# Weight casts ahead of the last square of a chunk, and the plain heads' values split at step 10

## The chip, the cores and the metric

The kernel runs on one core of a Trainium2 chip. The metric is the device time of one execution in microseconds (us). The core has five engines that run side by side and wait for each other through semaphores: TensorE (PE in the profile, its weight loads PEld), VectorE (DVE), ScalarE (ACT), GpSimd (POOL) and SyncE (SP), which here only issues the loads and stores (DMA). Each engine works through its own queue in order, so an instruction that waits holds up all that stands behind it on that engine.

## What is computed

One layer of a transformer block: a modulated norm, one input projection into three groups of heads (plain attention with grouped keys, a long convolution, differential attention), an output projection, and a gated feed-forward part, for 512 latent tokens and 256 context tokens of width 1024. Cut to what matters here:

```python
qa, ka, va, hy, qd, kd, vd = jnp.split(h @ w_in, IN_SPLITS, axis=-1)          # 512 latent rows
qa_c, ka_c, va_c, hy_c, qd_c, kd_c, vd_c = jnp.split(hc @ w_in, IN_SPLITS, axis=-1)  # 256 context rows
ka = apply_rope(rms_norm(ka.reshape(b, n, A_KV_HEADS, HEAD_DIM), kn_a), cos, sin)
qa = apply_rope(rms_norm(qa.reshape(b, n, A_HEADS, HEAD_DIM), qn_a), cos, sin)
ya = gqa_attention(qa, concat([ka_c, ka]), concat([va_c, va]))
yd = diff_attention(qd, concat([kd_c, kd]), concat([vd_c, vd]), lam)   # qd, kd normed and rotated alike
yh = hyena(hy, ...)
y = merge_groups(ya, yh, yd, g_out, w_out, lam_init)
x = x + g1 * y
x = x + g2 * conv_glu(modulate(rms_norm(x, norm2_g), sh2, sc2), w_up, ffn_conv_w, ffn_conv_b, w_down)
```

All is float32. The kernel keeps that accuracy by splitting each operand into a high half (a cast to the matmul's shorter type) and a low half (the operand minus the high half), and by three matmuls for one: high x high, high x low, low x high.

## The kernel before

**The projection.** The weights for queries, keys and values come as 16 units of 128x1024, two for each of eight chunks `ch`, in the order 0, 1, 4, 2, 3, 5, 6, 7 (`ci` counts them). A `Stream` (line 121) loads a unit raw (`wr`, three buffers, SP), casts its high half (`wh`, ScalarE, line 72) and subtracts its low half (`wl`, VectorE, line 80); high and low halves have two buffers each. `get(i)` (line 144) prepares units i and i+1 and loads the next two. So the call for the second half of a chunk prepares units 2ci+1 and 2ci+2, and unit 2ci+3 is prepared by the call at the start of the next chunk. Its buffer is the one of unit 2ci+1, which TensorE reads last in the last matmul of chunk ci.

A chunk fills two banks for the latent rows (`q0L` and so on) and, for keys and values, a third one for the context rows (`q3C`). After its matmuls each bank is evicted (lines 863 to 924): for queries and keys ScalarE squares it (`sq`, line 880) into one of four large buffers `b` that it shares with the rotation's products `ra`, `rb`; VectorE sums the square by head; POOL turns the sum into a reciprocal root and adds and scales the products. Chunks 6 and 7 and a part of 5 are values and are copied.

**Modulation columns.** Beside this, `mod2_step` (line 746) loads 512 KB pieces `mraw` and accumulates them on VectorE (`macc`, line 764); after eight pieces TensorE sums the columns (`mc`, line 769).

**Order of the instructions.** Outside the sections that fix it by hand, a scheduler chooses each engine's order from its own timeline, with the written order and any edges that are added as its limits. `tc.issue_after(ins)` adds such an edge: what is traced inside it comes behind `ins` on the same engine. In chunk 7 the order of TensorE and VectorE is fixed as written, and in the attention (line 1176) that of TensorE, VectorE and ScalarE.

**The attention.** Steps n from 3 to 28: four differential heads with four steps each (a step is 128 queries; its two score tiles of 128x768 are `jj` 0 and 1), then two blocks of plain heads. A step writes, in this order, the scores and maximum of `jj` 0, the mixing of the step before (`combine`: POOL scales and adds), a first `advance()`, the transposes, the exponential and the other half, the value matmuls of five steps before, and a second `advance()`. `advance()` takes each running generator one `yield` further: head preparation (`prepare`, started at the steps in `PREP_AT`), head finishing (`finish_d`), and `split_va` (line 946), which is started at step `VA_AT`. It casts the values of a plain head (`vas` from `va`, 128x768, ScalarE), yields, subtracts the low half on VectorE, yields, and does the same for the second head. The tiles take the place of `kd0` and `kd1`, the keys of the differential heads, which `prepare` reads for the last time in step 9. The score tiles have two buffers, so the scores of a step wait for the exponential of the same half in the step before.

Of the kernel before, what the change touches and what calls it, by code (L numbers as in the profile page):

```python
# [1 line left out]

# [8 lines left out]
AF = mybir.ActivationFunctionType  # L11
# [10 lines left out]
EARLY = 3  # L22
MOD_AT = (0, 0, 0, 2, 2, 2, 2, 2, 2, 2, 2, 2, 2, 2, 0, 0)
PREP_AT = (4, 7, 12, 17)
VA_AT = 13
HY_AT = (5, 6)
WO_AT = (24, 26, 28)
TAIL = (2, 0, 0, 0, 0, 0, 10, 0, 0, 4)
# [16 lines left out]
def block_kernel(tc, x, ctxt, small, ffs, wmod1, wmod2, whyd, wqkvd, woutd, wupd, wdownd,  # L45
                 fw1d, fw2d, fw3d, hbiasd, gains, identd, zTd, decayd, dftd, coefd, roped, out):
    nc = tc.nc
    V, S, G, T_ = nc.vector, nc.scalar, nc.gpsimd, nc.tensor
# [21 lines left out]
    def hi_of(dst, src, eng):  # L70
        if eng == "a":
            return S.copy(dst, src)  # L72
        elif eng == "v":
            V.tensor_copy(dst, src)
        else:
            G.tensor_scalar(dst, src, 1.0, 0.0, ALU.mult, ALU.add)

    def lo_of(dst, src, hi, eng):
        e = V if eng == "v" else G
        return e.tensor_tensor(dst, src, f(hi), ALU.subtract)  # L80
# [27 lines left out]
    def pa(name):  # L108
        return psB.tile([P, 512], F32, tag="a", bufs=3, name=name)
# [8 lines left out]
    def big(name):  # L118
        return tmp.tile([P, 1024], F32, tag="b", bufs=4, name=name)

    class Stream:
# [12 lines left out]
        def prep(self, i):  # L134
            if i < len(self.units) and i not in self.split:
                self.load(i)
                r = self.raw[i]
                h = self.pl.tile([P, 1024], F32R, tag=self.tag + "h", bufs=self.hb, name=f"{self.tag}h{i}")
                l = self.pl.tile([P, 1024], F32R, tag=self.tag + "l", bufs=self.hb, name=f"{self.tag}l{i}")
                hi_of(h, r, self.heng(i))  # L140
                lo_of(l, r, h, self.leng(i))
                self.split[i] = (h, l)

# [50 lines left out]
    def rstd_of(o, ss, n, k):  # L194
        G.tensor_scalar(o, ss, 1.0 / n, EPS, ALU.mult, ALU.add)
        G.tensor_tensor(o, o, mhalf[:, :k], ALU.pow)
# [615 lines left out]
    def early_mix(n):  # L812
        ml = cst.tile([P, 1], F32, tag="mle", bufs=2, name=f"mle{n}")
        mix(held[n], state["rr0"][:, n], state["st0"][:, n], ml)
# [3 lines left out]
    squ = Stream(wp, [wqkvd[2 * c_ + u] for c_ in corder0 for u in range(2)], lambda i: "a", lambda i: "v")  # L818
    corder = (0, 1, 4, 2, 3, 5, 6, 7)
    tabs = {}  # L820
    for ci, ch in enumerate(corder):
        kv = ch in (2, 3, 5, 6, 7)
        banks = [pa(f"q{ch}L0"), pa(f"q{ch}L1")] + ([pa(f"q{ch}C")] if kv else [])
        banks = [Bank(t) for t in banks]
        if ci == 6:
            for _ in prepare(0, pt):
                pass
        for u in range(2):
            for _ in range(MOD_AT[2 * ci + u]):
                mod2_step()  # L830
            if ci == 7 and u == 0:
                order = tc.manual_schedule(engines={mybir.EngineType.PE, mybir.EngineType.DVE})
                order.__enter__()
                nextp = prepare(1, pt)
            wh, wl = squ.get(2 * ci + u)
            wh, wl = (w.rearrange("p (k c) -> p k c", k=4) for w in (wh, wl))
            for b, bank in enumerate(banks):
                th, tl = (hTh, hTl) if b < 2 else (cTh, cTl)
                for j in range(2):
                    tt = (2 * b + j) if b < 2 else j  # L840
                    sl = slice(tt * P, (tt + 1) * P)
                    for kk in range(4):
                        k = 4 * u + kk
                        bank.mm3(bank.t[:, j * 256:(j + 1) * 256], th[:, k, sl], tl[:, k, sl], wh[:, kk], wl[:, kk],
                                 j == 1 and k == NK - 1)
                    if ci == 7:
                        e = 6 * u + 2 * b + j
                        if e % 2 == 0:
                            early_step(e // 2)
                        if e in (4, 8):  # L850
                            early_mix(e // 4 - 1)
                        if e in (2, 4, 6, 8, 9):
                            mod2_step()
                        if e > 3:
                            next(nextp, None)
            if ci == 7 and u == 1:
                for _ in nextp:
                    pass
                early_mix(EARLY - 1)
                while m2s["n"] < m2s["end"] or "due" in m2s:  # L860
                    mod2_step()
                order.__exit__(None, None, None)
        for b, bank in enumerate(banks):
            bank = bank.t
            lat = b < 2
            kt0 = 2 + 2 * b if lat else 0
            bv = bank.rearrange("p (j g d) -> p j g d", j=2, g=4)
            b2 = bank.rearrange("p (j c) -> p j c", j=2)

            if ch in (0, 1, 2, 3, 4, 5):  # L870
                ngr = 2 if ch == 5 else 4
                isq = ch in (0, 1, 4)
                w = ngr * 64
                ti = {0: 2, 1: 2, 2: 3, 3: 3, 4: 0, 5: 1}[ch]
                src = bv[:, :, :ngr, :]
                if ti not in tabs:
                    tabs[ti] = tables(ti)
                t512 = lambda nm: big(f"{nm}{ch}{b}")[:, :2 * ngr * 64].rearrange("p (j g d) -> p j g d", j=2, g=ngr)
                sq = t512("sq")
                S.activation(sq, src, AF.Square)  # L880
                s8 = tmp.tile([P, 2, ngr], F32, tag="s8", bufs=2, name=f"s8{ch}{b}")
                V.tensor_reduce(s8, sq, AX.X, ALU.add)
                r8 = tmp.tile([P, 2, ngr], F32, tag="r8", bufs=2, name=f"r8{ch}{b}")
                rstd_of(r8.rearrange("p j g -> p (j g)"), s8.rearrange("p j g -> p (j g)"), 64, 2 * ngr)
                if isq:
                    G.tensor_scalar(r8, r8, QK_SCALE, 0.0, ALU.mult, ALU.add)
                if isq:
                    dst = (qa[:, 2 * b:2 * b + 2, :] if ch == 4 else qd[:, 2 * b:2 * b + 2, ch * 256:(ch + 1) * 256])
                elif ch == 5:
                    dst = ka[:, kt0:kt0 + 2, :]  # L890
                else:
                    dst = kd[ch - 2][:, kt0:kt0 + 2, :]
                dst4 = dst.rearrange("p j (g d) -> p j g d", d=64)
                r4 = r8.rearrange("p j g -> p j g").unsqueeze(3).broadcast_to([P, 2, ngr, 64])
                if lat:
                    ra, rb = t512("ra"), t512("rb")
                    for tg, tab in zip((ra, rb), tabs[ti]):
                        tb = tab[:, 2 * b:2 * b + 2, :].unsqueeze(2).broadcast_to([P, 2, ngr, 64])
                        V.tensor_tensor(tg, src, tb, ALU.mult)
                    swp = rb.rearrange("p j g (i w) -> p (j g i) w", w=2)[:, :, ::-1]  # L900
                    ras = ra.rearrange("p j g (i w) -> p (j g i) w", w=2)
                    G.tensor_tensor(ras, ras, swp, ALU.add)
                    G.tensor_tensor(dst4, ra, r4, ALU.mult)
                else:
                    ra = t512("rc")
                    gb = gbc[:, ti, :].unsqueeze(1).unsqueeze(1).broadcast_to([P, 2, ngr, 64])
                    V.tensor_tensor(ra, src, gb, ALU.mult)
                    G.tensor_tensor(dst4, ra, r4, ALU.mult)
            if ch == 5:
                if b == 0:  # L910
                    for i in range(2):
                        t = vy.tile([P, 6, P], F32, name=f"va{i}")
                        G.memset(t, 0.0)
                        Vt.append(t)
                for i in range(2):
                    cs = slice(128 + 64 * i, 192 + 64 * i)
                    S.copy(Vt[i][:, kt0:kt0 + 2, 64 * i:64 * i + 64], b2[:, :, cs])
            if ch >= 6:
                if b == 0:
                    Vt += [vy.tile([P, 6, P], F32, tag=f"vd{ch}{i}", bufs=1, name=f"vd{ch}{i}") for i in range(2)]  # L920
                for i in range(2):
                    t = Vt[2 + 2 * (ch - 6) + i]
                    cs = slice(i * P, (i + 1) * P)
                    hi_of(t[:, kt0:kt0 + 2, :], b2[:, :, cs], "v" if i else "a")
# [198 lines left out]
    def start(g):  # L1123
        running.append(g)
# [53 lines left out]
    while n < len(steps) + D_V:  # L1178
        if n in WO_AT:
            wo_unit(WO_AT.index(n))  # L1180
        if n in PREP_AT:
            start(prepare(PREP_AT.index(n) + 2, ps_t))
        if n == VA_AT:
            start(split_va())
        if n in HY_AT:
            b = HY_AT.index(n)
# [336 lines left out]
```

## Time and profile before

| | us |
|---|---|
| median of three runs | 796.11 (795.91 to 796.15) |
| the profiled execution, its own time | 796.76 |
| its span, first to last instruction | 795.0 |
| TensorE busy in the span | 771.1 (97%) |
| VectorE / ScalarE / POOL busy | 475.6 / 318.2 / 193.8 |
| mean granted clock of TensorE | 0.993 |

The stages in the time of the span: filters and norms until about 55, the first projections and the long convolution until about 179, queries, keys and values from 103 to 264, the attention from 265 to 372, the output projection until about 420, the feed-forward part to the end.

Rows of the profile are read so: a row of the order in time has start, length, engine, line, operation, output <- inputs with their shapes, a count, and in brackets the idle time of the engine before it and what ended it. A row of the view of stages has the stretch, its length, the busy time of the engines (with numbers of instructions), the granted clock, the DMA engines' share and GB/s.

### The profile page before, as it was taken

Reading aid. Unit: us, or ns where it says so; the run is one execution under the profiler, and the core shown is the slowest. Engines: PE = TensorE matmul, PEld = TensorE weight load, DVE = VectorE, ACT = ScalarE, POOL = GpSimd, SP = SyncE. Lnnn points to the kernel's source line nnn. Section 1 sums busy time; section 2 is a strip of 40 time slices with the busy share of each in tenths; the row PEclk is TensorE's granted clock in tenths of the full one; section 3 lists DMA queues with packets and bytes.
Section 4 is the critical chain, followed back from the end, with each engine's and each line's share of the span. In section 5 each row is a group of like instructions: output and inputs, shape, how many; then the busy total and the mean of one; then the engine's idle time right before and its main releaser. Section 6 shows DMA issues by size and latency. Waiting matters only on the chain.

```text
span 795.0 us, 11146 instructions
## 1 busy us (share of the span) xinstructions
PE 771.1 (97%) x4355; PEld 654.2 (82%) x4355; DVE 475.6 (60%) x684; ACT 318.2 (40%) x546; POOL 193.8 (24%) x186
## 2 busy tenths in 40 slices
PE   7799999999999999999999999999999999999997
PEld 2278899999999888889889888888888888888886
DVE  5588659777776888786567774443444433333325
ACT  2576243222213688786343443233233232323220
POOL 0518026848831767340060000000000000000000
PEclk9899999999999999999999999999999999999999
DMA  8923311224685343311531552323323322323202
GB/s 328 395 58 111 106 54 55 80 80 160 213 226 160 92 107 76 97 54 50 209 116 54 204 171 102 107 80 106 106 80 106 103 84 79 108 81 105 84 23 106
DMA packets 30701, 93.68 MB, mean 118 GB/s; under 512 B 5639, under 2 KB 8022, under 8 KB 29625
## 3 DMA queue, kind: packets, MB, share of 16 engines
q1 hardware_dynamic: 30649, 92.98, 35.4%
q8 instruction: 34, 0.56, 0.3%
q14 instruction: 18, 0.15, 0.1%
HBM read 83.79 MB, written 2.10 MB: 108 GB/s over the span
## 4 chain that ended last, share of the span: by engine, by line
PE 84%; DVE 5%; DMA 4%; ACT 3%; POOL 2%; issue 1%; SPq 0%; DVEq 0%; ACTq 0%; POOLq 0%
PE u L84 5%; PE u L85 5%; PE u L83 5%; PE dn L85 5%; PE dn L84 5%; PE dn L83 5%; DMA mraw<-in_dram 4%; PE uv L83 2%; PE ua L85 2%; PE uv L84 2%; PE uv L85 2%; PE ua L83 2%; PE ua L84 2%; PE yd L1111 2%; PE o L85 2%; PE o L84 2%
## 5 line engine op out<-in xcount | busy, mean ns | idle before, releaser
L80 DVE TENSOR_TENSOR ul<-ur,uh 128x1024 fp32r<-128x1024 f32 x62 | 75.9, 1224 | 101.1 <-ACT uh L72 100.4
L72 ACT CAST uh<-ur 128x1024 fp32r<-128x1024 f32 x66 | 69.1, 1051 | 117.9 <-PE u L84 90.6
L83 PE MATMUL u<-h2h,uh 128*128 128x512 f32 (+1 forms) x224 | 81.2, 363 | 0.0
L85 PE MATMUL u<-h2h,ul 128*128 128x512 f32 (+1 forms) x224 | 80.3, 359 | 0.0
L84 PE MATMUL u<-h2l,uh 128*128 128x512 f32 (+1 forms) x224 | 80.3, 359 | 0.0
L84 PE MATMUL dn<-ul,gh 128*128 128x512 f32 x176 | 69.6, 396 | 0.0
L85 PE MATMUL dn<-uh,gl 128*128 128x512 f32 x176 | 69.6, 396 | 0.0
L83 PE MATMUL dn<-uh,gh 128*128 128x512 f32 x176 | 69.3, 396 | 0.0
L80 DVE TENSOR_TENSOR gl<-gT,gh 128x512 fp32r<-128x512 f32 x22 | 15.2, 689 | 60.1 <-ACT gh L72 60.1
L84 PEld LDWEIGHTS u<-h2l,uh 128*128 128x128 f32 x224 | 42.3, 189 | 6.2
L83 PEld LDWEIGHTS u<-h2h,uh 128*128 128x128 f32 x224 | 42.3, 189 | 6.2
L85 PEld LDWEIGHTS u<-h2h,ul 128*128 128x128 f32 x224 | 42.3, 189 | 6.2
L80 DVE TENSOR_TENSOR wl<-wr,wh 128x1024 fp32r<-128x1024 f32 x22 | 31.6, 1434 | 19.3 <-ACT wh L72 19.2
L764 DVE SCALAR_TENSOR_TENSOR macc<-mraw,sv,macc 128x1024 f32<-128x1024 f32 x28 | 38.0, 1358 | 6.3 <-DMA mraw<-in_dram 6.2
L72 ACT CAST gh<-gT 128x512 fp32r<-128x512 f32 x22 | 13.5, 620 | 70.1 <-PE dn L84 70.1
L85 PEld LDWEIGHTS dn<-uh,gl 128*128 128x128 f32 x176 | 33.2, 188 | 8.1
L83 PEld LDWEIGHTS dn<-uh,gh 128*128 128x128 f32 x176 | 33.1, 188 | 8.1
L84 PEld LDWEIGHTS dn<-ul,gh 128*128 128x128 f32 x176 | 33.1, 188 | 8.1
L72 ACT CAST wh<-wr 128x1024 fp32r<-128x1024 f32 x22 | 23.0, 1048 | 41.3 <-PE hy L84 8.2
L83 PE MATMUL uv<-h2h,uh 128*128 128x512 f32 x80 | 31.2, 390 | 0.2 <-ACT uh L72 0.2
L83 PE MATMUL ua<-h2h,uh 128*128 128x512 f32 x80 | 31.3, 392 | 0.0
L84 PE MATMUL uv<-h2l,uh 128*128 128x512 f32 x80 | 31.2, 390 | 0.0
(771 smaller groups left out, 2167.3 us busy)
## 6 DMA issues: line engine op xcount, KB each, us to landing
ur<-in_dram SPq DMA_DIRECT2D x66, 512.0 KB, 3.2
mraw<-in_dram SPq DMA_DIRECT2D x32, 512.0 KB, 4.2
wr<-in_dram SPq DMA_DIRECT2D x22, 512.0 KB, 3.3
mraw<-in_dram SPq DMA_DIRECT2D x8, 1024.0 KB, 11.7
or<-in_dram SPq DMA_DIRECT2D x8, 512.0 KB, 4.3
xo<-in_dram SPq DMA_DIRECT2D x6, 512.0 KB, 9.1
x<-in_dram SPq DMA_DIRECT2D x4, 512.0 KB, 7.3
out_dram<-x SPq DMA_DIRECT2D x8, 256.0 KB, 2.0
```

Of the source, the lines that this page charges most:

```text
L72: return S.copy(dst, src)
L80: return e.tensor_tensor(dst, src, f(hi), ALU.subtract)
L83: i0 = T_.matmul(o, ah, bh, start=start, stop=False)
L84: T_.matmul(o, ah, bl, start=False, stop=False)
L85: return i0, T_.matmul(o, al, bh, start=False, stop=stop)
L764: V.scalar_tensor_tensor(m2s["a"], r, sv[:, k:k + 1], m2s["a"], ALU.mult, ALU.add)
L1111: T_.matmul(o, Vt[2 + h][:, kt], at[:, kt], start=kt == 0, stop=kt == 5)
```

## The change

The change does two things. It prepares unit 2ci+3 right after the matmuls of chunk ci, ahead of that chunk's evictions, and puts the square of the chunk's last bank behind that unit's cast in ScalarE's queue. And it starts `split_va` at step 10 instead of step 13.

```diff
-VA_AT = 13
+VA_AT = 10
...
-                hi_of(h, r, self.heng(i))
+                self.last = hi_of(h, r, self.heng(i))
                 lo_of(l, r, h, self.leng(i))
...
                 order.__exit__(None, None, None)
+
+        squ.prep(2 * ci + 3)
         for b, bank in enumerate(banks):
...
                 sq = t512("sq")
-                S.activation(sq, src, AF.Square)
+                with (tc.issue_after(squ.last.ins) if b == len(banks) - 1 else contextlib.nullcontext()):
+                    S.activation(sq, src, AF.Square)
```

The high half, the low half, the loads and the squares are the same instructions as before; none is added and none is left out. For the last chunk there is no unit 17, and the new line does nothing.

More of the change, by code (lines that the diff above doesn't have):

```diff
@@ L1 @@
+import contextlib
 import math
```

## The prediction

> **What bounds the kernel now.** I read the page first, then a table of stages, then the rows around each idle piece of TensorE.
>
> ```profile
> PE 84%; DVE 5%; DMA 4%; ACT 3%; POOL 2%; issue 1%; SPq 0%; DVEq 0%; ACTq 0%; POOLq 0%
> ```
>
> This is the page's chain that ended last: TensorE is the bound, so the change can win only what TensorE idles near the moved work, and loses whatever new idling it makes. The view of stages gives that idling (length, then busy time of PE, PEld, DVE, ACT, POOL; granted clock; DMA share and GB/s):
>
> ```profile
> 197.00:201.10 4.10, 2.85 (x25) 2.65 (x24) 2.58 (x4) 1.53 (x2) 3.93 (x5) 1.00 0.57 207
> 201.10:235.00 33.90, 32.34 (x273) 32.16 (x273) 25.96 (x31) 7.40 (x17) 21.62 (x21) 1.00 0.76 226
> 293.00:306.00 13.00, 12.82 (x73) 10.49 (x73) 10.67 (x22) 10.90 (x24) 11.20 (x9) 1.00 0.28 66
> 306.00:322.00 16.00, 13.62 (x84) 11.47 (x83) 13.40 (x25) 12.44 (x28) 9.74 (x9) 1.00 0.56 155
> 233.40:236.80 3.40, 1.84 (x18) 1.83 (x17) 2.04 (x3) 0.00 (x0) 0.10 (x1) 1.00 0.48 157
> 236.80:240.40 3.60, 3.60 (x20) 3.60 (x20) 2.12 (x3) 0.00 (x0) 0.00 (x0) 0.53 0.62 223
> ```
>
> Length minus PE: 1.25 us idle at 197 to 201 (a weight cast), 1.56 in the next stage, 0.18 in steps 10 to 12 of the attention, 2.38 in steps 13 to 16. The first and the last belong to the two edits: 3.63 us together, 0.46% of the median 796.11, is all that they can win directly. The last two rows matter for a rival.
>
> **Part one: the casts.** Six chunks have squares; in each the high half of unit 2ci+3 is now issued on ScalarE ahead of the last bank's square. Nothing is added: each cast, its low half on VectorE and its load are the old instructions, the load had been issued already by the older call, so SP's queue gets no new entry. The one place where this order held TensorE is the end of chunk `ch` 3, the fifth in order (the order in time of ScalarE, TensorE, VectorE and POOL, one after the other):
>
> ```profile
> 199.51 0.60 ACT L880 ACTIVATE sq<-q3C 128x512 f32<-128x512 f32 x1 [4.73 <-POOL ra L902]
> 200.00 1.04 ACT L72 CAST wh<-wr 128x1024 fp32r<-128x1024 f32 x1
> ```
>
> ```profile
> 196.72 0.28 PE L85 MATMUL q3C<-wh,cTl 128*128 128x256 f32 x1
> ...
> 199.56 0.28 PE L85 MATMUL q5L<-wh,hTl 128*128 128x256 f32 x1
> 201.09 0.50 PE L83 MATMUL q5L<-wh,hTh 128*128 128x256 f32 x2 [1.25 <-ACT wh L72]
> ```
>
> ```profile
> 198.04 0.68 DVE L899 TENSOR_TENSOR rb<-q3L,sg 128x512 f32<-128x512 f32 x1
> ...
> 202.73 2.31 DVE L80 TENSOR_TENSOR wl<-wr,wh 128x1024 fp32r<-128x1024 f32 x1
> ```
>
> ```profile
> 198.19 1.29 POOL L902 TENSOR_TENSOR ra<-ra,rb 128x512 f32<-128x512 f32 x1
> ```
>
> The square waited 4.73 us for POOL to release its buffer, and the cast stood behind it, though the cast needed only the matmul that ended at 196.72 + 0.28 = 197.00. Put first, it runs 197.0 to 198.05; TensorE wants it at 199.56 + 0.28 = 199.84, so the 1.25 goes. What is late next is the low half: VectorE is free at 198.04 + 0.68 = 198.7, but POOL's add holds it (part two shows how) to 199.48, so it ends at about 199.5 + 1.1 = 200.6 (an estimate from the row at 60.41 below, where half as many elements took 0.55 after POOL) instead of 202.73 + 2.31 = 205.04. If the scheduler puts a low-half matmul at 199.96, TensorE waits 0.65 there and the gain is 0.6; with TensorE's order as it is (one early matmul, then other banks), 1.25. I take 1.25, the row's own value, and keep 0.6. The square itself stays behind POOL, at 199.5. At the other five chunk ends it comes one cast (1.04 us) later and delays only the head norms; the list of waits names none of TensorE at the first four of these ends, and the results are read by transposes much later; were that cover gone, one cast, 1.04, would be the price at one end. At the end of chunk 6 there is no square, only the cast and a shorter copy that change places; I take 0.
>
> Does the 1.25 reach the end? The next idle piece is the second sum of modulation columns:
>
> ```profile
> 211.39 0.17 DVE L770 TENSOR_TENSOR mcol<-mc,cols 128x8 f32<-128x8 f32 x1 [1.86 <-PE mc L769]
> ...
> 233.57 1.28 DVE L764 SCALAR_TENSOR_TENSOR macc<-mraw,sv,macc 128x1024 f32<-128x1024 f32 x1 [0.86 <-DMA mraw<-in_dram]
> ```
>
> ```profile
> 235.00 1.92 PE L769 MATMUL mc<-ones,macc 128*128 128x2 f32 x16 [1.56 <-DVE macc L764]
> ```
>
> TensorE waits at 235.00 for a chain of loads and multiply-adds. That chain starts after 211.39, which itself waited for TensorE (the first sum), so it starts 1.25 earlier too, and I carry the gain through. If it were paced by its loads alone, all 1.25 would be given back here; this is the upper end, 0.
>
> **Part two: the plain heads' values.** Two high casts (ScalarE) and two low halves (VectorE) leave steps 13 and 14 and join 10 and 11. The loads, matmuls and transposes stay where they are. First what they cost in the old place (ScalarE, TensorE, VectorE):
>
> ```profile
> 308.82 0.81 ACT L72 CAST vas<-va 128x768 fp32r<-128x768 f32 x1
> ...
> 319.58 0.90 ACT L784 ACTIVATE pd33None<-sd33None,mxd33None 128x768 f32<-128x768 f32 x1 [2.94 <-DVE rrd L787]
> ```
>
> ```profile
> 310.95 0.51 PE L777 MATMUL sd32None<-ksX,X 128*128 128x512 f32 x1 [0.73 <-ACT pd31None L784]
> ...
> 320.99 0.66 PE L975 MATMUL yTd<-ident,ynd 128*128 128x128 f32 x4 [1.65 <-ACT atd30None L72]
> ```
>
> ```profile
> 311.53 0.95 DVE L80 TENSOR_TENSOR vas<-va,vas 128x768 fp32r<-128x768 f32 x1
> 312.50 0.96 DVE L781 TENSOR_REDUCE mxd32None<-sd32None 128x1 f32<-128x768 f32 x1
> ...
> 317.55 0.95 DVE L80 TENSOR_TENSOR vas<-va,vas 128x768 fp32r<-128x768 f32 x1
> 318.53 0.96 DVE L781 TENSOR_REDUCE mxd33None<-sd33None 128x1 f32<-128x768 f32 x1
> ```
>
> The first cast stands ahead of the exponential for which TensorE waits 0.73. Both low halves stand ahead of the maximum at 318.53, ScalarE idles 2.94 for it, and TensorE's 1.65 hang on that exponential. Without them the maximum comes 0.97 + 0.98 = 1.95 earlier, and so do the exponential and the transposes at 320.99: 319.04. TensorE, 0.73 earlier itself, arrives at 320.99 - 1.65 - 0.73 = 318.61 and still waits 0.4. So -1.95 of the 2.38.
>
> Now the new place, where the first low half is queued right behind `ynd` and ahead of the maximum at 298.64 (VectorE, ScalarE, POOL, TensorE):
>
> ```profile
> 297.75 0.69 DVE L1007 TENSOR_TENSOR ynd<-ynd,s4d 128x512 f32<-128x512 f32 x1
> 298.64 0.96 DVE L781 TENSOR_REDUCE mxd23None<-sd23None 128x1 f32<-128x768 f32 x1 [0.20 <-PE sd23None L778]
> ```
>
> ```profile
> 299.69 0.90 ACT L784 ACTIVATE pd23None<-sd23None,mxd23None 128x768 f32<-128x768 f32 x1 [0.25 <-DVE rrd L787]
> ```
>
> ```profile
> 297.79 2.34 POOL L790 TENSOR_TENSOR pd21None<-pd21None,pd21None 128x768 f32<-128x768 f32 x1
> ```
>
> ```profile
> 301.13 0.59 PE L777 MATMUL sd30None<-ksX,X 128*128 128x512 f32 x1
> ```
>
> The second cast (0.81) fits ScalarE's queue: at 299.69 it waits for VectorE already, and that wait only grows below; the first has the same cover a step earlier, and were it gone, 0.8 would be the price. The low half reads two SBUF tensors, and so does POOL's add, which runs to 297.79 + 2.34 = 300.13. How such a pair shares is in these rows of an early stage (VectorE, then POOL):
>
> ```profile
> 59.81 0.69 DVE L324 TENSOR_TENSOR fpdm<-sd 128x512 f32<-128x512 f32 x1
> 60.41 1.78 DVE L324 TENSOR_TENSOR fpdp<-sd 128x512 f32<-128x512 f32 x1
> ```
>
> ```profile
> 60.02 1.62 POOL L80 TENSOR_TENSOR hTl<-hm,hTh 128x512 fp32r<-128x512 f32 x1 [3.96 <-ACT hTh L72]
> ```
>
> Two like operations on `sd` follow each other on VectorE; POOL's came between their starts, went ahead of the second, and the second took 1.78 instead of 0.69, ending 0.55 after POOL's end at 61.64. So POOL's waiting add at 297.79 goes before the low half: that runs from 300.13 and the maximum starts near 301.0 instead of 298.64, 2.4 later. The exponential at 299.69 ended at 300.59; it ends near 303.0, and the scores at 301.13, which take over its buffer, start there: TensorE idles some 1.85 that it does not idle now. If VectorE kept its place instead, the maximum would be 0.6 late, TensorE under 0.2. By the row I take +1.85; ends 0.2 and, with the second low half held up as well, 2.9 (one more wait like that at 60.41, 1.1). Part two is then -1.95 + 1.85 = -0.1. [...]
>
> **Sum.** -1.25 - 0.1 = -1.35 against the profiled execution's own 796.76, which gives 795.41; that execution lies 0.65 over the median 796.11 of the runs, so 794.76, said as **794.8**.
>
> **Rivals.**
> 1. *VectorE keeps its place behind `ynd`*, or POOL's add comes late enough: part two is -1.95 + 0.2 = -1.75, the sum -3.0: **793.1**. For it: POOL's request at 297.79 is only 0.65 ahead of the low half's (297.75 + 0.69 = 298.44). Against: the row at 60.41.
> 2. *The cast's gain is given back at 235.00*, the loads being the pace: only -0.1 is left, **796.0**; with the second low half held up as well, **797.1**. For it: VectorE waits for a load just before.
> 3. *The wait at 235.00 goes with the reordering.* The 1.56 wait and the sums after it leave TensorE nearly idle for 3.4 us (233.40 to 236.80), and the following 3.6 us ran at a granted 0.53, which costs 3.6 x 0.47 = 1.7. Both gone: -3.25 more, **791.5**. Against: the edit doesn't touch the loads. [...]
> 4. *Slower: TensorE's order now trusts the low half.* TensorE's order here is the scheduler's. With the high half ready at 198.05 it may queue unit 11's low-half matmuls at 199.96, while VectorE still does other work first and ends the low half at 205.04 as now. Then TensorE waits 5.1 instead of 1.25, +3.85, plus rival 3's slow stretch, 1.7, and part two's -0.1: 796.11 + 5.45, **801.6**. It decides from about 203 on: a low half that ends there makes the kernel 1.6 slower. Against: it is not behind the square any more.
> 5. *The change does nothing*: the cast could be held by its raw tile or its buffer. Both are free at 197.0, so I give it little.
>
> **How the numbers follow.** Forecast case 45%, by itself 794.3 (the 0.4 that TensorE still waits at 319.04 gone too) to 795.4 (0.6 for the cast); rival 1 17%, rival 2 13% (its 797.1 included), rival 3 9%, rival 4 11%, the rest mixtures. A measurement tells 0.2%, 1.6 us, from no change: faster means under 794.5. About a third of the forecast case and rivals 1 and 3 lie there: 0.42. Slower, over 797.7, is rival 4 with a little of the rest: 0.12. Within: 0.46. The range 791.9 to 797.2 reaches from just short of rival 3 to the upper end of rival 2.
>
> **What would show it.** Right: unit 11's cast starts near 197.0 and TensorE has no wait on it; no `vas` row between 306 and 322 and under 0.5 idle there; a low half of `vas` that takes over 2 us in step 10, and a new wait of the scores `sd30` near 303. A low half of 0.95 and no such wait speaks for rival 1, a longer wait at the second sum for rival 2, full clock after it for rival 3, a wait on `wl` in q5 for rival 4. I am wrong above all if the scheduler reorders more of 110 to 250 than this one cast.

## The result and the profile after

The changed kernel takes 805.53 us (median of 16 runs, 802.15 to 807.25) against 797.57 for the kernel before (16 runs, 795.59 to 804.82, taken beside it). The ratio is 1.0090 with a 95% interval of 1.0075 to 1.0106: it is slower by 0.9%, some 7 to 8 us, where 1.35 us less was forecast. The profiled execution took 805.08 with a span of 803.3 and a mean clock of 0.985 (before 796.76, 795.0 and 0.993).

**Where the time went.** The view of one tile's instructions gives the start of the first and the last matmul (or transpose) of a kind, so two such rows side by side tell how far TensorE lies behind at that place. Before:

```profile
L83 PE MATMUL q3L<-wh,hTh x32: 279/281/285, 179.8 to 193.6; 128*128 128x256 f32 x32
L83 PE MATMUL q6L<-wh,hTh x32: 279/281/367, 218.2 to 232.2; 128*128 128x256 f32 x32
L83 PE MATMUL q7L<-wh,hTh x32: 274/281/365, 240.5 to 260.0; 128*128 128x256 f32 x32
L777 PE MATMUL sd12None<-ksX,X x4: 280/378/580, 277.2 to 279.6; 128*128 128x512 f32 x2, 128*128 128x256 f32 x2
L777 PE MATMUL sd20None<-ksY,qsY x4: 280/378/580, 285.5 to 287.5; 128*128 128x512 f32 x2, 128*128 128x256 f32 x2
L777 PE MATMUL sd30None<-ksX,X x4: 280/380/587, 301.1 to 303.7; 128*128 128x512 f32 x2, 128*128 128x256 f32 x2
L975 PE MATMUL yTd<-ident,ynd x16: 271/273/328, 302.0 to 344.8; 128*128 128x128 f32 x16
```

After (lines moved by one, and by four from line 880 on):

```profile
L84 PE MATMUL q3L<-wh,hTh x32: 279/281/285, 179.5 to 193.4; 128*128 128x256 f32 x32
L84 PE MATMUL q6L<-wh,hTh x32: 279/281/362, 221.1 to 235.1; 128*128 128x256 f32 x32
L84 PE MATMUL q7L<-wh,hTh x32: 274/281/415, 245.1 to 264.4; 128*128 128x256 f32 x32
L778 PE MATMUL sd12None<-ksX,X x4: 280/380/585, 285.4 to 287.8; 128*128 128x512 f32 x2, 128*128 128x256 f32 x2
L778 PE MATMUL sd20None<-ksY,qsY x4: 280/378/580, 293.7 to 295.8; 128*128 128x512 f32 x2, 128*128 128x256 f32 x2
L778 PE MATMUL sd30None<-ksX,X x4: 280/379/499, 311.2 to 313.6; 128*128 128x512 f32 x2, 128*128 128x256 f32 x2
L979 PE MATMUL yTd<-ident,ynd x16: 272/273/329, 312.0 to 353.1; 128*128 128x128 f32 x16
```

The lag is -0.3 us at the first `q3L`, +2.9 at `q6L`, +4.6 at `q7L`, +8.2 at `sd12` and `sd20`, +10.1 at `sd30`, and +8.3 at the last `yTd`. So there are three losses ahead of `sd20` (3.2 in q5, 1.7 around the second column sum, 3.6 early in the attention), and the second part of the change loses 1.9 up to `sd30` and wins 1.8 after it. How the first two divide varies from one execution to another: by the same rows, with TensorE's order unchanged, the three are 0.5, 3.0 and 4.4 in the profile of e1 below and 3.6, 1.7 and 3.8 in that of e2. The waits of TensorE after, from 60 to 400 us (in all, how often, the longest), say on what:

```profile
PE sd10None L778 <- ACT pd03None L785: 3.0, 1, 3.0
PE mc L770 <- DVE macc L765: 2.7, 1, 2.7
PE q5L L84 <- DVE rb L903: 2.6, 2, 2.2
PE sd30None L778 <- ACT pd23None L785: 1.5, 1, 1.5
PE yTd L979 <- ACT atd30None L73: 1.0, 1, 1.0
```

Before, the one at `sd10` was

```profile
PE sd10None L777 <- ACT pd03None L784: 0.9, 1, 0.9
```

Unit 11's cast, which held q5 before, is gone from the list after. Behind each of the first three waits stands a stretch at a lower granted clock: 0.77, 0.66 and 0.72 (view of stages, the clock is the first figure after the five busy times). Before, only the second place had one, 3.6 us at 0.53:

```profile
200.00:205.00 5.00, 2.77 (x15) 2.59 (x14) 5.00 (x6) 0.00 (x0) 4.92 (x4) 0.77 0.56 184
240.00:250.00 10.00, 9.29 (x52) 9.24 (x53) 6.67 (x10) 3.29 (x4) 0.16 (x1) 0.66 0.59 194
270.00:280.00 10.00, 6.94 (x31) 5.89 (x31) 3.78 (x10) 5.10 (x11) 5.14 (x6) 0.72 0.01 2
```

Length times what the clock lacks of 1.00, an estimate of the price from these rows, is 1.2 us in q5, 3.4 around the second column sum (before 1.7) and 2.8 in the attention. Beside the three waits, which are 1.3, 1.1 and 2.1 longer than before's, that is most of the rest of the first loss and more than the rest of the other two.

**First cause: SP's queue.** SP's order in time before,

```profile
169.81 0.33 SPq L131 DMA_DIRECT2D wr<-in_dram  x1
170.20 0.89 SPq L759 DMA_DIRECT2D mraw<-in_dram  x2
183.51 0.33 SPq L131 DMA_DIRECT2D wr<-in_dram  x1
```

and after, with the row of SP's waits that explains it:

```profile
169.55 13.92 SPq L132 DMA_DIRECT2D wr<-in_dram  x2
183.52 1.67 SPq L760 DMA_DIRECT2D mraw<-in_dram  x2
...
SPq L132 <- DVE wl L81: 15.3, 3, 13.2
```

The load of weight unit 12 waits until 183 us for a raw buffer that a low half frees. Before, the first two loads of the column sums went out ahead of it, at 170.20; after, they stand behind it and go out at 183.52, 13.3 us late. The load of unit 12 itself is no later than before (183.51); what changed is what stands behind it. The first sum on VectorE starts at 188.75 instead of 183.40, three more wait for their loads on the way into q5, and what stands between them on VectorE is late too (VectorE, then TensorE, after):

```profile
188.75 0.84 DVE L763 TENSOR_SCALAR macc<-mraw,sv 128x1024 f32<-128x1024 f32 x1 [4.44 <-DMA mraw<-in_dram]
...
199.66 2.13 DVE L765 SCALAR_TENSOR_TENSOR macc<-mraw,sv,macc 128x1024 f32<-128x1024 f32 x1 [0.32 <-DMA mraw<-in_dram]
201.71 0.68 DVE L903 TENSOR_TENSOR rb<-q3L,sg 128x512 f32<-128x512 f32 x1
```

```profile
202.54 0.38 PE L84 MATMUL q5L<-wh,hTh 128*128 128x256 f32 x1 [2.23 <-DVE rb L903]
```

`rb` is the last reader of a bank that q5 takes over. It ran at 198.04 before and at 201.71 now, behind the late sums; the one just ahead of it waited 0.32 for its load and took 2.13 instead of 1.28.

**Second cause: an address.** ScalarE's first copy of the attention (before, then after) and POOL's third early mix (after):

```profile
267.07 0.48 ACT L72 COPY atd00None<-Td00None 128x384 f32<-128x384 f32 x1 [0.67 <-ACT pe L784]
```

```profile
274.36 0.48 ACT L73 COPY atd00None<-Td00None 128x384 f32<-128x384 f32 x1 [3.52 <-POOL pe L791]
...
272.52 1.80 POOL L791 TENSOR_TENSOR pe<-pe,pe 128x768 f32<-128x768 f32 x1
```

The copy has nothing to do with the third mix. It waits because the attention's pool is opened over the memory of the projection's temporaries, and the scheduler gives out the four large buffers `b` of these in the order in which they come free on its own timeline. These are the bytes of a partition in the compiled programs (names as in the code, e1 to e12 are the experiments below):

```
                   atd00 at           lies over
before, e6, e9     48256 to 54400     kh of job 1, qhl of job 1
after, e1, e3      48256 to 54400     qhl of job 1, pe21 (52032 to 56128)
e4, e5, e7, e10    56448 to 62592     kh of job 1, pe11
e8, e12            48256 to 54400     pe11, qhl of job 1
e11                56448 to 62592     pe21 (56128 to 60224), pe11
```

`pe21` is an operand of the third mix. A buffer that landed elsewhere became a wait of 3.52 us.

**The edge.** The change adds an edge that puts the square behind the cast. The compiled program without that edge, with the early preparation alone, has the same order on every engine: it is the earlier place in the written order that moves everything.

### The profile page after: what moved, and what is told of

It reads as the page before. It is cut to its first block, busy times and chain, and to the rows that moved or that the text cites. A ratio compares the mean times of both kernels' runs of the same rounds, so it can differ in the third digit from the quotient of the medians.

```text
span 803.3 us, 11142 instructions
## 1 busy us (share of the span) xinstructions
PE 774.9 (96%) x4355; PEld 659.1 (82%) x4355; DVE 478.2 (60%) x684; ACT 318.3 (40%) x546; POOL 190.0 (24%) x186
## 4 chain that ended last, share of the span: by engine, by line
PE 83%; DVE 6%; DMA 5%; ACT 2%; issue 1%; SPq 1%; POOL 0%; DVEq 0%; ACTq 0%; POOLq 0%
DMA mraw<-in_dram 5%; PE u L84 5%; PE u L85 5%; PE u L86 5%; PE dn L86 5%; PE dn L85 5%; PE dn L84 5%; PE uv L84 2%; PE ua L86 2%; PE uv L86 2%; PE uv L85 2%; PE ua L84 2%; PE ua L85 2%; PE o L86 2%; PE o L85 2%; PE o L84 2%
```

## The experiments

Each is shown against the kernel before on the same chip, as median and ratio with its 95% interval.

**e1 and e2: the casts alone.**

```diff
-VA_AT = 10
+VA_AT = 13
```

> The change without its second part: the casts as in the change, the values split at step 13 as before. Theory A (all of the loss comes from the first part: in the trace of after TensorE lies 0.3 us ahead of before at the first q3L, 2.9 behind at the first q6L, 4.6 at the first q7L, 4.4 at sd03, 8.2 at sd12, and again 8.3 at the end): 7.5 to 9 us over the kernel before, about 805.5. The prediction on record (the first part gains 1.25): 796. Theory B (the second part carries the loss, 10.1 us late at sd30): within 1 us of the kernel before.

> The same kernel a second time, as a look at how far two runs of it agree: within 0.3% of e1_casts under every theory.

Measured: e1 806.49 (6 runs) against 797.73, ratio 1.0101 (1.0077 to 1.0126); e2, the same kernel again, 805.34, ratio 1.0083 (1.0054 to 1.0113). The whole loss is in the first part, theory A; theory B falls.

**e3: SP's order put back.** From e1:

```diff
-        dma(r, wmod2[g, k])
+        ins = dma(r, wmod2[g, k])
+        if n == 1:
+            m2s["dma"] = ins
...
-            wh, wl = squ.get(2 * ci + u)
+            with (tc.issue_after(m2s["dma"].ins) if (ci, u) == (4, 1) else contextlib.nullcontext()):
+                wh, wl = squ.get(2 * ci + u)
```

> The casts as in e1, with one SP entry put back: the load of unit 12 (which waits for a low half's buffer until 183.15 in the trace of after) behind the second load of the modulation sums, as before. The order on TensorE, VectorE, ScalarE and GpSimd is that of e1, instruction for instruction. Theory A1 (the loads of the sums, 13.3 us late at 183.52 instead of 170.20, cause the waits in q5 and ahead of mc, 3.2 + 1.7 us by the lags at q6L and q7L): 4 to 6 us under e1, 800 to 802. Rival A2 (the new order on VectorE and TensorE in q5 does it, whatever the loads do): no change, 805 to 806. The wait of 3.5 us of ScalarE's atd00 copy on GpSimd stays under both.

Measured: 802.78 against 797.56, ratio 1.0076 (1.0052 to 1.0100), 2.6 to 3.7 us under e2 and e1 by the medians (these ran on another chip) and less than expected; the intervals overlap, so this pair alone doesn't settle it. The trace does what A1 says (SP's order in time): the first loads of the sums go out at 170.47 again,

```profile
170.08 0.33 SPq L132 DMA_DIRECT2D wr<-in_dram  x1
170.47 0.89 SPq L760 DMA_DIRECT2D mraw<-in_dram  x2
```

and q5 has no wait on `rb` among TensorE's, with the order on TensorE and VectorE unchanged from e1. The wait at `sd10` is still 3.0 us.

**e4: the layout alone, and e5: both.** From e1, and from e3:

```diff
     att = pool("att")
+    att.tile([P, 1024], F32R, tag="qk", bufs=2, name="qkpad")
```

> The casts as in e1, and the attention's SBUF tiles laid out in another order (the two unstacked-query buffers ahead of the three of the transposed probabilities), so that the first of those, atd00, does not lie over the buffer of the third early mix, pe21. Every engine's order is that of e1. Theory A3 (ScalarE's 3.5 us wait for GpSimd at 274, and TensorE's 3.0 us with the half clock behind it, come from these addresses alone; lag 4.4 to 8.2 us): 3 to 4 us under e1, about 802. Rival A4 (the wait follows from GpSimd's being late, and something else holds sd10 as long): under 1 us gained.

> e3 and e4 together. Theory A1 with A3: both costs gone, what is left is the first part by itself: the kernel before less the 1.25 us of the prediction, 796 to 798. If the costs overlap (a wait removed early is met again at sd10 or at mc): 798 to 802. Rivals A2 and A4: over 802.

Measured: e4 802.58, ratio 1.0062 (1.0039 to 1.0084); e5 798.32, ratio 1.0009 (0.9994 to 1.0025). Between e4 and e5 only the SP entry differs, and the intervals lie apart: 4.3 us by the medians. Between e3 and e5 only the layout differs, and they lie apart too: 4.5 us. So both causes are shown, each worth 4.3 to 4.5 us where the other is gone already (some 3 to 4 us by the medians where it is not, e3 and e4 against e2 and e1), and together they are the whole loss. A2 and A4 fall. In e4 the wait at `sd10` is what it was before the change:

```profile
PE q5L L84 <- DVE rb L903: 1.8, 2, 1.3
...
PE sd10None L778 <- ACT pd03None L785: 0.9, 1, 0.9
```

But e5 is no faster than the kernel before, though q5's 1.25 should now be won. Its waits of TensorE:

```profile
PE mc L772 <- DVE macc L767: 3.7, 1, 3.7
...
PE q5L L84 <- DVE rb L906: 0.6, 1, 0.6
```

Half of q5's wait is still there, now on `rb`, and the wait ahead of the second column sum, 1.6 before, is 3.7. The first comes from the sum ahead of `rb` (VectorE, e3, then e5):

```profile
197.56 1.28 DVE L767 SCALAR_TENSOR_TENSOR macc<-mraw,sv,macc 128x1024 f32<-128x1024 f32 x1
```

```profile
197.70 2.31 DVE L767 SCALAR_TENSOR_TENSOR macc<-mraw,sv,macc 128x1024 f32<-128x1024 f32 x1 [0.33 <-DMA mraw<-in_dram]
```

In e3, where every engine's order is the same, it took 1.28 and q5 had no wait; in e5 it waited 0.33 for its load and took 2.31. That POOL's add `ra` ran beside it and stretched it, like the pair that the prediction reads at 60.41, is the author's inference.

**e6: the second part alone.** The kernel before with `VA_AT = 10`.

> The second part alone: the kernel before with the plain heads' values split at step 10. Prediction on record: -0.1 (+1.85 at sd30, -1.95 at sd32, yTd and the last max), 797.5; by the lags in the trace of after (8.2 at sd20, 10.1 at sd30, 8.3 at the end) the two ends are +1.9 and -1.8. Rival (the low halves delay step 10 and nothing is won later): 799 to 800.

Measured: 798.71 against 797.56, ratio 1.0018 (0.9998 to 1.0039): no difference that these runs can tell, with a hint of a loss. The waits of TensorE from 290 to 330 have the forecast's two ends, 1.8 at `sd30` against 1.0 at `yTd`:

```profile
PE sd30None L777 <- ACT pd23None L784: 1.8, 1, 1.8
PE yTd L975 <- ACT atd30None L72: 1.0, 1, 1.0
```

**e7: SP's order put back further.** From e5: the edge also puts the load of unit 14 behind the eighth load of the sums.

```diff
-            with (tc.issue_after(m2s["dma"].ins) if (ci, u) == (4, 1) else contextlib.nullcontext()):
+            af = {(4, 1): 1, (5, 1): 7}.get((ci, u))
+            with (tc.issue_after(m2s["dma", af].ins) if af else contextlib.nullcontext()):
                 wh, wl = squ.get(2 * ci + u)
```

> e5 with one more SP entry put back: the load of unit 14 behind the eighth load of the modulation sums, as before. Every other engine's order is that of e1. Theory A5 (with both costs gone the first part still earns nothing, 798.3, because the weights' load that went ahead of the eighth sum's load keeps the sums late: the second mc begins at 238.41 in e5 and at 235.00 before): the second mc by 236, the wait ahead of it 2 us or less, 795.5 to 797. Rival A6 (the sums are paced by their own transfers and buffers, and what q5 gains is lost again ahead of mc in any order): as e5, 798, with mc's wait near 3.7.

Measured: 798.24, ratio 1.0008 (0.9991 to 1.0024), as e5. The second `mc` begins at 236.8 with a wait of 2.4, between the two theories; the time is A6's. One profile can't decide here: with the order of before up to this place the wait is 1.6 before, 0.7 in e6 and 2.1 in e9. Nor is SP's order that of before throughout: the sixth load of the second sum still goes out behind three transfers of the head preparation, at 221.98 instead of ahead of them by 220.6, so theory A6 is tested only up to there.

**e8: unit 11's casts alone.** From e1:

```diff
-        squ.prep(2 * ci + 3)
+        if ci == 4:
+            squ.prep(2 * ci + 3)
...
-                with (tc.issue_after(squ.last.ins) if b == len(banks) - 1 else contextlib.nullcontext()):
+                with (tc.issue_after(squ.last.ins) if b == len(banks) - 1 and ci == 4 else contextlib.nullcontext()):
```

> Before, with the first part for chunk q3 alone: only the casts of unit 11 (the one whose lateness TensorE waits for, 1.3 us in q5) is issued ahead of the square of q3C; the other chunks and the split at step 13 as before. In this program the load of unit 12 stands behind the first two loads of the sums by itself, and atd00 does not lie over pe21. The prediction's first step (1.25 us of q5's wait gone): q5's wait under 0.3, 796 to 797; if the gain is given back ahead of mc, as in e5: 797.5 to 798.5. Against theory A (the two side effects are the loss): over 800.

Measured: 797.12 against 797.14, ratio 0.9992 (0.9977 to 1.0008). The loss is gone without any repair: with the other chunks left alone, unit 12's load stays behind the sums' first loads and `atd00` misses `pe21`. No wait in q5 is left, and TensorE reaches q7 58.1 us after the first `q3L` (238.8 - 180.7), against 60.7 before; but with the order of before this stretch is 58.4 in e6 and 61.3 in e9, so one profile proves little. This execution lost 2 us again in the attention, where `yTd` waited 1.94 and the clock fell behind it:

```profile
318.00:322.00 4.00, 2.06 (x12) 1.73 (x11) 2.71 (x7) 2.84 (x7) 2.33 (x2) 0.85 0.80 266
322.00:326.00 4.00, 4.00 (x21) 3.40 (x21) 2.11 (x3) 2.07 (x5) 3.11 (x3) 0.72 0.03 11
```

**e9: the values split clear of POOL's add, and e10: with e7.** From before, and from e7:

```diff
-    def split_va():
-        for j in range(2):
+    def split_va(j):
+        if True:
...
-        if n == VA_AT:
-            start(split_va())
+        if n in (11, 12):
+            start(split_va(n - 11))
```

> Before, with the plain heads' values split in two places, value 0 at step 11 and value 1 at step 12, so that neither low half begins beside the add of GpSimd that the low half of step 10 waited for (2.58 us in e6 instead of 0.95). If the collision with the add is what cancels the gain of the second part: TensorE's 1.8 us wait at sd30 gone, the waits at sd32 (0.7) and yTd (1.6) shorter, 0.5 to 1.9 us gained, 795.7 to 797. Rival (any low half in these steps holds a max as long): 797 to 799.

> e7 and e9 together: the sum of the two, 794 to 796.5 if each does what its theory says; 798 to 799 if A6 and the rival of e9 hold.

Measured: e9 796.36 against 797.14, ratio 0.9988 (0.9970 to 1.0005); e10 797.33, ratio 0.9997 (0.9981 to 1.0012). In e9 the wait at `sd30` is gone, `yTd` waits 1.0, and a new one of 0.9 stands at `Td21`, on ScalarE's copy behind the moved cast. By the medians the gain is about 1 us, but the interval includes none. e10 missed: the two small terms don't show beside the wait ahead of `mc`, 3.2 in its profile.

**e11: the address alone, the other way round.** The kernel before with e4's one line.

> The kernel before with the layout line of e4 alone, every engine's order as before. There the buffers of the early probabilities are handed out otherwise, and this line puts atd00 over pe21 (its bytes 56448 to 62592 over 56128 to 60224), where it lay clear of it. Theory A3 (the overlap alone costs 3 to 4 us): ScalarE's atd00 copy waits 2 to 4 us for GpSimd's third early mix, TensorE waits some 2 to 3 us at sd10, 800 to 802. Rival (the layout of e4 helps as such, or the overlap costs only where all is late): 796 to 798.

Measured: 801.30 against 797.78, ratio 1.0042 (1.0023 to 1.0061). ScalarE and TensorE in order of time:

```profile
270.87 0.48 ACT L72 COPY atd00None<-Td00None 128x384 f32<-128x384 f32 x1 [3.52 <-POOL pe L790]
```

```profile
272.91 0.50 PE L777 MATMUL sd10None<-ksX,X 128*128 128x512 f32 x1 [3.60 <-ACT pd03None L784]
```

The line that saves 4 us in the changed kernel costs 3.5 in the kernel before, with no engine's order changed in either: it is the address and nothing else.

**e12: e8 and e9 together.**

> e8 and e9 together: unit 11's casts alone ahead of q3C's square, and the values split at steps 11 and 12. If the two small gains of e8 (0.0) and e9 (0.8) add: 795.5 to 797; if what q5 gains is lost ahead of mc again and the second part's gain with it: 797 to 798.5.

Measured: 794.60 (11 runs, 792.19 to 796.43) against 797.78, ratio 0.9957 (0.9939 to 0.9976): 3.4 us faster than the kernel before, under the expected 795.5 to 797, and about 11 faster than the changed one. It is more than e8 and e9 add up to (0.0020), though within their intervals. Its waits of TensorE from 190 to 330 begin with

```profile
PE mc L770 <- DVE macc L765: 1.8, 1, 1.8
PE yTd L980 <- ACT atd30None L73: 1.0, 1, 1.0
PE Td21None L1099 <- ACT atd20None L73: 0.9, 1, 0.9
```

and the clock stays at 1.00 from 314 to 334. That the shorter wait at `yTd` keeps what q5 won, which e8's execution lost there, is the likely reason; no run shows it apart.

## Why the prediction was wrong

**The step that failed** is in part one: "Nothing is added: each cast, its low half on VectorE and its load are the old instructions, the load had been issued already by the older call, so SP's queue gets no new entry." No entry is new, but an old one moved. In VectorE's order the low half of unit 9 stands two places earlier than before (it runs from 180.80 to 183.12, ahead of the sum `s` and the product `rc`, instead of from 182.26 to 183.48 behind them), and unit 12's load, which takes the raw buffer that this low half frees, went ahead of the sums' loads. That the one follows from the other is inferred from the two orders; that the load's place costs the time is measured. The prediction looked only at the load of the unit being cast, and not at the next load that the same buffer releases. e5 against e4 prices this at 4.3 us. The other chunk ends, which were costed at nothing because TensorE waits for nothing there, are where it comes from: with unit 11's edit alone (e8) it doesn't happen. No run separates which of them moved the load; unit 9's low half points to the end of chunk `ch` 2.

**What no step had** is the address. The prediction asked which instruction waits for which, and took the buffers as given; they are handed out along the scheduler's timeline, so a reordering among the projections changed what a tile of the attention, written at 267, lies over. e5 against e3 gives 4.5 us, e11 3.5.

**The cast itself**: right. It runs at 196.76 (forecast 197.0), ahead of the square (ScalarE, after), and TensorE doesn't wait for it:

```profile
196.76 1.05 ACT L73 CAST wh<-wr 128x1024 fp32r<-128x1024 f32 x1 [2.05 <-PE q3C L86]
199.33 0.60 ACT L884 ACTIVATE sq<-q3C 128x512 f32<-128x512 f32 x1 [1.51 <-POOL ra L906]
```

The low half came later than 200.6: VectorE reached it only at 202.31, behind the sum and `rb`. It cost nothing by itself, since TensorE's order did not trust it, and rival 4, a wait on `wl`, did not come. The slower outcome is larger than this rival's (5.45) and came by another mechanism.

**Whether 1.25 reaches the end**: it was carried through, and in e5 and e7 it is lost. Both stand at the time of the kernel before, where rival 2 put it; their profiles show a longer wait at the second column sum, as that rival says. With unit 11 alone q5 has no wait left, and the time shows a gain once the second part is placed well (e12). Rival 3 called TensorE nearly idle from 233.40 to 236.80; its own row has it busy for 1.84 of these 3.40 us, so the clock fell there, to 0.53, behind a wait of 1.56 and a short busy stretch, not behind 3.4 us of idling. That a shorter wait spares the slow stretch fits one profile, e6, where TensorE waited 0.7 for that sum and the clock from 235 to 240 was 1.00 (before 0.71); no run tests it apart.

**Part two**: its two ends were right in sign and nearly in size; their balance, -0.1, is less than the runs can tell, and e6's hint is of a loss. The first low half went behind POOL's add as forecast (VectorE, then POOL, after):

```profile
306.57 2.59 DVE L81 TENSOR_TENSOR vas<-va,vas 128x768 fp32r<-128x768 f32 x1
309.09 0.94 DVE L782 TENSOR_REDUCE mxd23None<-sd23None 128x1 f32<-128x768 f32 x1
```

```profile
306.01 2.35 POOL L791 TENSOR_TENSOR pd21None<-pd21None,pd21None 128x768 f32<-128x768 f32 x1
```

It took 2.59 instead of 0.95 and ended 0.8 after the add, and TensorE waited 1.46 at `sd30`, 1.75 in e6, for the 1.85 of the sum. By the lags the two ends are +1.9 and -1.8, for +1.85 and -1.95, so their balance is +0.1 instead of -0.1. Like the pair at 60.41, where the second of two like operations took 1.78 instead of 0.69, the operation that began behind POOL's ended behind it. Rival 1 falls.

**The warning**, that the scheduler might reorder more of 110 to 250 than this one cast, named the right danger. It carried no price: the chance of slower, 0.12, came almost wholly from rival 4, and the range ended at 797.2.

## What to carry to other kernels

Where a scheduler orders the instructions, moving one piece of work earlier moves the buffers it frees, and with them the loads that wait for these buffers (here they went out 13.3 us late): read the order of the queue that issues the loads, before and after, ahead of any sum over engines. A pool that is opened over freed memory inherits waits from whatever lay there (here 3.52 us), and which tile that was can change with any reordering upstream; a wait on work that has no part in the data is the sign of it, and laying out the tiles in another order is a one-line test. Make the smallest edit that reaches the stall (one unit, not six), and place an operation clear of one on another engine beside which it runs long (the low half beside POOL's add took 2.59 us here instead of 0.95).

## What the runs showed of the hardware

In these runs the granted clock after a short wait did not follow from the length of the wait alone. TensorE waited 1.94 us for `yTd` in e8 and the clock fell to 0.72 in a stretch behind it; it waited 1.93 in e3 at the same instruction, and the clock fell to 0.75 behind it; it waited 1.93 in e1 and kept 1.00 (rows of the view of stages around the wait, e1):

```profile
326.00:330.00 4.00, 2.07 (x15) 1.76 (x14) 2.71 (x7) 2.74 (x7) 2.22 (x2) 1.00 0.76 265
330.00:334.00 4.00, 4.00 (x28) 3.64 (x27) 2.13 (x3) 3.60 (x8) 3.23 (x3) 1.00 0.02 7
```
